# Computing two thirds of a mixer's gate projections inside another stage and passing them through DRAM

## The chip, the cores and the metric

The kernel runs on one core of a Trainium2 chip. The metric is the device time of one execution in microseconds (us): here the median of repeated runs.

## The reference

The reference is one inference step of a decoder trunk of two layers, for a prompt of 512 tokens and 8 single sample tokens, together 520 columns. A layer has a mixer with three parallel branches (retention, HGRN2, Mamba-2 SSD), merged by gates, and then a squared-ReLU MLP. What matters here:

```
proj = xn @ w_in                       # one big input projection, its last 3 x 1024 columns are the gates
...                                    # y_r, y_h, y_m: outputs of the three branches, 1024 wide each
ys     = stack([y_r, y_h, y_m])
branch = einsum('blnw,nwd->blnd', ys, w_branch)
gate   = sigmoid(gates.reshape(B, L, 3, 1024))
merged = sum(gate * branch, axis=2)
return merged @ w_out
```

A gate depends on the normalized input `xn` alone, and not on its branch, so that it can be computed at any time after `xn` and before its branch product.

## The kernel before

Activations are kept transposed: 128 features on the partitions, 520 tokens along the free axis, eight such blocks for 1024 features. Each float32 operand is held as two parts, high and low (`XN`, `YB`, and each weight); `mm3` (L209) makes a product from high x high, high x low and low x high, in two pieces of 256 and 264 columns. So one projection of 128 output features is 8 x 3 x 2 = 48 matmuls and needs one weight block of 512 KB. `wload` (L157) loads a block into one of four raw buffers and splits it in four pieces, each with one copy on ScalarE (L173) and one subtraction on VectorE (L174), into two ready pairs. The order of all weight uses is written down ahead in a list (L1190 and on), and `weights` (L182) starts loads up to four uses ahead.

`pj` (L233) gives a projection one of two accumulators in PSUM. The tile pool `up` has 18 buffers (tiles named `u`), shared by nearly all intermediate tiles of 128 x 520. The instructions of each engine are put in order before the run by a scheduler that goes by a model of time and by the order of the program; on the chip each engine, and SyncE's queue of transfers (SP), takes them in that fixed order.

One layer runs through these stages:

1. HGRN, eight heads. `hg_unit` (L487) is a generator of ten pieces. The first four start with a projection each: the forget gate (its exponentials follow), the query (ends at L561), the value (taken over at L580) and the output gate (L596). The other six (the products L630, the running state L632 and L634, the output L646, and so on) are issued as tails between the pieces of the next heads: `unit` (L270) runs one piece of the new head and then `step()` runs one piece of every tail.
2. SSD, four groups (`ssd_unit`, six pieces with a projection each, and six of tail).
3. `branch(l, 1, "first")` (L1080): for each of eight blocks, `gate` (L1072) projects the gate and takes it over with a tanh on ScalarE (L1074), then the branch product from `YB`, then gate times product on VectorE (L1090) into `T2`. Both halves end with a `step()`.
4. Retention, four heads (`ret_unit`, six pieces with a projection each, and four of tail), with the normalization of the SSD output as a tail.
5. `branch(l, 2, "mid")`: as 3, but the product is added to `T2` on GpSimd.
6. Eight gates of the first branch into `T1`, `branch(l, 0, "last")`, the output projection, the MLP.

Of the kernel before, what the change touches and what calls it, by code (L numbers as in the profile page):

```python
# [10 lines left out]
F32 = mybir.dt.float32  # L11
F32R = mybir.dt.float32r
U8 = mybir.dt.uint8
AF = mybir.ActivationFunctionType
ALU = mybir.AluOpType

P = 128
D = 1024
NB = 8
SEQ = 512  # L20
NS = 8
T = SEQ + NS
# [13 lines left out]
C_Z, C_XBC, C_DT, C_GATE = 7168, 8192, 10240, 10256  # L36
# [53 lines left out]
def hybrid_step(ctx: ExitStack, tc: tile.TileContext, x_prompt, x_sample, state_ret, state_hgrn, state_ssm,  # L90
# [5 lines left out]
    V, S, G, PE, SY = nc.vector, nc.scalar, nc.gpsimd, nc.tensor, nc.sync  # L96
# [7 lines left out]
    dp = ctx.enter_context(tc.tile_pool(name="dp", bufs=3, space=bass.MemoryType.DRAM))  # L104
# [5 lines left out]
    def nm(s):  # L110
        uid[0] += 1
        return f"{s}{uid[0]}"

    def ut(dt=F32):
        return up.tile([P, UW], dt, tag="u", name=nm("u"))[:, :T]
# [93 lines left out]
    def mm3(ps, w, ah, al, halves=(0, 1), m=P, ks=range(NB)):  # L209
        hi, lo = w  # L210
        for k in ks:
            for wt, act, st, sp_ in ((hi, ah, k == 0, False), (hi, al, False, False), (lo, ah, False, k == NB - 1)):
                for h in halves:
                    PE.matmul(ps[:m, CH[h]], lhsT=wt(k), rhs=act[:, k, CH[h]], start=st, stop=sp_)  # L214
# [18 lines left out]
    def pj():  # L233
        t = psj.tile([P, 1024], F32, tag="pj", name=nm("pj"))
        return t[:, 512 - CUTS[1]:512 - CUTS[1] + T]
# [6 lines left out]
    def w_cols(l, c0, n=128):  # L242
        return w_in[l, :, c0:c0 + n]

    def proj(l, c0, n=128):
        if (l, c0) in begun:
            ps = begun.pop((l, c0))
            mm3(ps, weights(w_cols(l, c0, n)), *XN, halves=(1,))
            return ps
        ps = pj()  # L250
        if (l, c0) in early:
            raw = early.pop((l, c0))
            mm3(ps, weights(w_cols(l, c0, n)), *YB, halves=(1,))
            scaled(raw, ps, 1)
            return raw
        mm3(ps, weights(w_cols(l, c0, n)), *XN, m=n)
        return ps
# [3 lines left out]
    def step():  # L261
        for g in list(tails):
            if next(g, "end") == "end":
                tails.remove(g)
# [2 lines left out]
        while tails:  # L267
            step()

    def unit(g, n):  # L270
        for _ in range(n):
            next(g)
            step()
        tails.append(g)

    def split(dst, val, scale=None, eng=None):
# [795 lines left out]
    def gate(l, b, d, dst):  # L1072
        ps = proj(l, C_GATE + 1024 * b + 128 * d)
        S.activation(out=dst, in_=ps, func=AF.Tanh, scale=0.5)  # L1074
        step()

    def w_br(l, b, d):
        return w_branch[l, b, :, 128 * d:128 * d + 128]

    def branch(l, b, mode):  # L1080
        for d in range(NB):
            if mode == "last":
                t = T1[:, d, :]
            else:
                t = ut()
                gate(l, b, d, t)
            ps = pj()
            mm3(ps, weights(w_br(l, b, d)), *YB)
            dst = T2[:, d, :] if mode == "first" else ut()
            V.scalar_tensor_tensor(out=dst, in0=t, scalar=1.0, in1=ps, op0=ALU.add, op1=ALU.mult)  # L1090
            if mode == "mid":
                G.tensor_tensor(out=T2[:, d, :], in0=T2[:, d, :], in1=dst, op=ALU.add)  # L1092
            elif mode == "last":
                V.tensor_tensor(out=dst, in0=T2[:, d, :], in1=dst, op=ALU.add)
                split((XN[0][:, d, :], XN[1][:, d, :]), dst, 0.5)
            step()
# [43 lines left out]
    def w_o(l, d):  # L1140
        return w_out[l, :, 128 * d:128 * d + 128]
# [7 lines left out]
    def hg_cols(h):  # L1149
        return [c + 128 * h for c in (C_HF, C_HQ, C_HI, C_HG)]  # L1150
# [18 lines left out]
    def add(src, n=128, store="w", start=None):  # L1169
        key = (str(src), len(key_info))  # L1170
        key_info[key] = (src, n, store if n == 128 else f"w{n}")
        fence[key] = len(uses) if start is None else start
        order.append(key)
        use(key)
        return key

    def use(key):
        first.setdefault(key, len(uses))
        last[key] = len(uses)
        uses.append(key)  # L1180
# [8 lines left out]
    for l in range(depth):  # L1189
        held = {}  # L1190
        for i, c in enumerate(early_cols if l else early_cols[:2]):
            held[c] = add(w_cols(l, c), store="wu"[i % 2] if l else "w")
        for h in range(HH):
            if h == HH - 1:
                add(w_cols(l, C_DT, 16), 16)
            for c in hg_cols(h):
                use(held[c]) if c in held else add(w_cols(l, c))
        for g in range(SG):
            for c in (C_XBC + 1024 + 128 * g, C_XBC + 1536 + 128 * g, C_XBC + 256 * g, C_XBC + 256 * g + 128,
                      C_Z + 256 * g, C_Z + 256 * g + 128):  # L1200
                add(w_cols(l, c))
        for d in range(NB):
            add(w_cols(l, C_GATE + 1024 + 128 * d))
            add(w_br(l, 1, d))
        for h in range(RH):
            for c in (C_RK + 128 * h, C_RQ + 128 * h, C_RV + 256 * h, C_RV + 256 * h + 128, C_RG + 256 * h,
                      C_RG + 256 * h + 128):
                add(w_cols(l, c))
        for d in range(NB):
            add(w_cols(l, C_GATE + 2048 + 128 * d))  # L1210
            add(w_br(l, 2, d))
        for d in range(NB):
            add(w_cols(l, C_GATE + 128 * d))
        for d in range(NB):
            add(w_br(l, 0, d))
        halves_order([w_o(l, d) for d in range(NB)], "y")
        for gi in range(4):
            held = {}
            for blocks, halves in up_order(gi):
                for i, d in enumerate(blocks):  # L1220
                    if halves == (1,) and d >= NUP - 4:
                        use(held[d])
                    else:
                        held[d] = add(w_u(l, gi, d), store="wu"[i % 2] if len(halves) == 1 else "w")
            if gi == 3:
                halves_order([w_d(l, gi, d) for d in range(NB)], "x")
            else:
                for d in range(NB):
                    add(w_d(l, gi, d))
# [18 lines left out]
    for c, (xt, (_, n)) in enumerate(zip(xts, rows)):  # L1248
# [9 lines left out]
        for i in range(2):  # L1258
# [3 lines left out]
            ps = pm()  # L1262
# [41 lines left out]
    for l in range(depth):  # L1304
        p = prms[l]
# [4 lines left out]
        else:  # L1310
            spare = [T2[:, i, :] for i in (0, 2, 7, 1)]
            for i, c in enumerate(early_cols):
                raw = spare[i]
                ps = pj()
# [8 lines left out]
        for h in range(HH):  # L1323
            if h == HH - 1:
                unit(ssd_dt(l, p, dtp), 1)
            unit(hg_unit(l, h, p), 4)
            if h == 1:
                G.memset(RR, 0.0)
        for g in range(SG):
# [22 lines left out]
        for gi in range(4):  # L1352
            for blocks, halves in up_order(gi):
                if gi == 0 and halves == (1,):
                    drain()
                for d in blocks:
                    ps = pj()
                    mm3(ps, weights(w_u(l, gi, d)), *XN, halves=halves)
                    c = slice(0, T) if len(halves) == 2 else CH[halves[0]]
                    n = c.stop - c.start  # L1360
                    a, t = ut()[:, :n], ut()[:, :n]
# [4 lines left out]
            for halves in ((0,), (1,)) if gi == 3 else ((0, 1),):  # L1366
                if gi == 3:
                    h = halves[0]
# [58 lines left out]
```

## Time and profile before

| | us |
|---|---|
| median of 3 runs | 2853.94 |
| lowest, highest | 2852.61, 2860.72 |
| profiled execution, its own time | 2847.65 |
| span of the profile | 2845.9 |

The span runs from the first to the last instruction in the trace; the profiled execution's own time is 1.75 us longer. In the stages named below, layer 0 has HGRN at 60 to 345 us, SSD at 345 to 538, the branch products of the second branch up to about 637; layer 1 has HGRN from about 1440 to 1740. PE is TensorE's matmul, PEld its weight load, DVE VectorE, ACT ScalarE, POOL GpSimd, SP the queue of SyncE.

### The profile page before, as it was taken

What the parts mean: (1) busy time and instruction counts of PE and PEld (TensorE: products, weight loads), DVE (VectorE), ACT (ScalarE), POOL (GpSimd) and SP (SyncE); (2) the same over time, 40 slices, a digit from 0 to 9 for tenths busy, and PEclk for the clock granted to TensorE, in tenths of its full rate; (3) what the DMA queues carried; (4) which work ended last, traced back from release to release, by engine and by line L of the source; (5) the groups of instructions that cost most, each with busy time, mean ns of one, the idle gap of its engine ahead of it and who ended that gap; (6) DMA issues with size and microseconds to landing.
All of it is one profiled execution on the core that took longest, in us unless ns stands there. A gap on an engine that the chain in (4) does not pass through costs nothing. (4 is left out here: it accounts for less than half of the span.)

```text
span 2845.9 us, 56632 instructions
## 1 busy us (share of the span) xinstructions
PE 2742.3 (96%) x22489; PEld 2652.0 (93%) x22489; DVE 1700.2 (60%) x3714; ACT 1168.6 (41%) x2858; POOL 738.1 (26%) x939
## 2 busy tenths in 40 slices
PE   5999899999999999999989999999999999999999
PEld 5888899999999999999978888999999999899998
DVE  4666799837654453443576668997476435534444
ACT  3444455424323353332444445553343234433333
POOL 2555443302211031000145554352022100300004
PEclk8999999999999999999999999999999999999999
DMA  5433355734543432333323333565354435133331
GB/s 145 118 102 103 88 143 149 179 90 122 162 126 96 123 87 80 96 90 90 109 70 106 106 107 93 140 171 147 90 156 133 123 95 149 45 97 90 95 97 63
DMA packets 597594, 317.99 MB, mean 112 GB/s; under 512 B 94385, under 2 KB 580273, under 8 KB 597201
## 3 DMA queue, kind: packets, MB, share of 16 engines
q1 hardware_dynamic: 596688, 314.21, 39.6%
q8 instruction: 178, 2.92, 0.4%
q14 instruction: 88, 0.71, 0.1%
q0 software_dynamic: 640, 0.15, 0.0%
HBM read 278.89 MB, written 35.41 MB: 110 GB/s over the span
## 5 line engine op out<-in xcount | busy, mean ns | idle before, releaser
L214 PE MATMUL pj<-XH,w 128*128 128x256 f32 (+1 forms) x8896 | 1529.7, 288 | 18.8 <-ACT T L580 6.0
L214 PEld LDWEIGHTS pj<-XH,w 128*128 128x128 f32 x8896 | 1268.7, 190 | 43.6 <-issue 10.9
L173 ACT ACTIVATE w<-wr 128x256 fp32r<-128x256 f32 (+1 forms) x1552 | 517.0, 404 | 1085.2 <-PE pj L214 1010.9
L214 PE MATMUL pj<-XL,w 128*128 128x256 f32 (+1 forms) x4448 | 947.2, 288 | 5.4 <-DVE XL L357 3.3
L174 DVE TENSOR_TENSOR w<-wr,w 128x256 fp32r<-128x256 f32 (+1 forms) x1552 | 630.7, 461 | 376.4 <-ACT w L173 375.8
L214 PEld LDWEIGHTS pj<-XL,w 128*128 128x128 f32 x4448 | 709.3, 190 | 19.4 <-issue 10.7
L214 PE MATMUL pj<-YH,w 128*128 128x256 f32 (+1 forms) x3456 | 575.4, 284 | 3.0 <-ACT YH L356 1.3
L214 PEld LDWEIGHTS pj<-YH,w 128*128 128x128 f32 x3456 | 487.6, 189 | 8.9 <-ACT w L173 3.4
L214 PE MATMUL pj<-YL,w 128*128 128x256 f32 (+1 forms) x1728 | 365.0, 284 | 2.5 <-DVE YL L357 2.4
L214 PEld LDWEIGHTS pj<-YL,w 128*128 128x128 f32 x1728 | 275.0, 189 | 5.0 <-DVE YL L357 4.0
L317 POOL TENSOR_TENSOR u<-u,u 128x256 f32<-128x256 f32 (+1 forms) x56 | 47.0, 840 | 567.7 <-ACT u L316 567.6
L1362 DVE SCALAR_TENSOR_TENSOR u<-pj,RR 128x520 f32<-128x520 f32 (+2 forms) x74 | 46.1, 625 | 171.8 <-PE pj L214 169.8
L933 POOL TENSOR_TENSOR u<-u,cst 128x520 f32<-128x520 f32 x16 | 22.0, 1376 | 292.8 <-ACT u L932 282.8
L1379 POOL TENSOR_SCALAR T<-T,gn 128x256 f32<-128x256 f32 (+1 forms) x16 | 16.0, 1003 | 298.9 <-ACT u L313 298.9
L1374 DVE TENSOR_TENSOR T<-T,pj 128x520 f32<-128x520 f32 x32 | 22.3, 696 | 115.3 <-PE pj L214 115.3
L287 PE MATMUL pm<-ident,u 128*128 128x128 f32 (+3 forms) x320 | 49.7, 276 | 20.5 <-DVE u L1260 20.4
L1092 POOL TENSOR_TENSOR T<-T,u 128x520 f32<-128x520 f32 x16 | 27.2, 1700 | 132.8 <-DVE u L1090 132.8
L287 PEld LDWEIGHTS pm<-ident,u 128*128 128x128 f32 (+3 forms) x320 | 37.3, 145 | 22.5 <-DVE u L1260 10.9
L287 PE MATMUL pm<-ident,T 128*128 128x128 f32 (+1 forms) x368 | 56.5, 281 | 1.3 <-DVE u L1134 1.0
L625 POOL TENSOR_TENSOR u<-u,s 128x512 f32<-128x512 f32 x32 | 37.5, 1188 | 66.5 <-DMA u<-in_state_hgrn_dram 52.8
L738 POOL TENSOR_TENSOR u<-u,u 128x544 f32<-128x544 f32 x32 | 45.7, 1428 | 34.5 <-DVE u L737 29.8
L648 ACT ACTIVATE u<-pm 128x512 f32<-128x512 f32 x16 | 9.5, 596 | 108.7 <-PE pm L646 108.7
(320 smaller groups left out, 3394.3 us busy)
## 6 DMA issues: line engine op xcount, KB each, us to landing
wr<-in_w_in_dram SPq DMA_DIRECT2D x208, 512.0 KB
wr<-in_w_up_dram SPq DMA_DIRECT2D x66, 512.0 KB
wr<-in_w_down_dram SPq DMA_DIRECT2D x64, 512.0 KB
u<-rbd SPq DMA_DIRECT2D x96, 256.0 KB
wr<-in_w_branch_dram SPq DMA_DIRECT2D x48, 512.0 KB
out_dram<-u SPq DMA_DIRECT2D x72, 256.0 KB
out_dram<-u SPq DMA_DIRECT2D x72, 128.0 KB
u<-in_state_hgrn_dram SPq DMA_DIRECT2D x32, 256.0 KB
```

What stands on the lines that cost most here:

```text
L173: a = S.activation(out=hi, in_=rq, func=AF.Copy)
L174: b = V.tensor_tensor(out=lo, in0=rq, in1=hi.bitcast(F32), op=ALU.subtract)
L214: PE.matmul(ps[:m, CH[h]], lhsT=wt(k), rhs=act[:, k, CH[h]], start=st, stop=sp_)
L287: PE.transpose(out, in_, ident[:k, :k])
L317: (eng or V).tensor_tensor(out=acc, in0=acc, in1=sq, op=ALU.add)
L625: G.tensor_tensor(out=c3(sts[i]), in0=c3(sts[i]), in1=bc(fs[:, s0, None], shc), op=ALU.mult)
L738: G.tensor_tensor(out=c, in0=c, in1=e, op=ALU.add)
L933: G.tensor_tensor(out=b, in0=b, in1=cst[:, K_SIN:K_SIN + T], op=ALU.mult)
L1092: G.tensor_tensor(out=T2[:, d, :], in0=T2[:, d, :], in1=dst, op=ALU.add)
L1362: V.scalar_tensor_tensor(out=a, in0=ps[:, c], scalar=0.0, in1=RR[:, c], op0=ALU.max, op1=ALU.mult)
L1374: V.tensor_tensor(out=T2[:, d, :], in0=T2[:, d, :], in1=ps, op=ALU.add)
L1379: G.tensor_scalar(out=T2[:, d, CH[h]], in0=T2[:, d, CH[h]], scalar1=p["fpost"][:, d:d + 1], scalar2=None, op0=ALU.mult)
```

## The change

The gates of the second and third branch (16 projections in each layer) are no longer computed in `branch`. They are computed in the HGRN stage: after the second and after the fourth piece of each head (with a few moved by one head in layer 1, where the first head uses another source for its projections). Each goes from PSUM through the tanh into a `u` tile and from there by a transfer of SP into a tile in DRAM. `branch` reads it back by a transfer of SP into a `u` tile in the place where it computed it. The list of weight uses follows. `branch` has one `step()` for each block in these two calls, where it had two.

```diff
-    def unit(g, n):
-        for _ in range(n):
+    def unit(g, n, after=None):
+        for i in range(n):
             next(g)
             step()
+            if after:
+                after(i)
         tails.append(g)
...
+    gates = {}
+
+    def gates_at(l, h, i):
+        at = {0: (3,), 1: (0, 1, 3)}.get(h, (1, 3)) if l else (1, 3)
+        n = 2 * h - (l > 0 and h == 1)
+        return [(1 + g // NB, g % NB) for g in (n + k for k, x in enumerate(at) if x == i)]
+
+    def gate_ahead(l, b, d):
+        ps = proj(l, C_GATE + 1024 * b + 128 * d)
+        t = ut()
+        S.activation(out=t, in_=ps, func=AF.Tanh, scale=0.5)
+        gates[l, b, d] = kept = dp.tile([P, T], F32, tag="gate", name=nm("gate"), bufs=2 * NB)
+        SY.dma_start(out=kept, in_=t)
+
...
             else:
                 t = ut()
-                gate(l, b, d, t)
+                SY.dma_start(out=t, in_=gates[l, b, d])
             ps = pj()
...
-            for c in hg_cols(h):
+            for i, c in enumerate(hg_cols(h)):
                 use(held[c]) if c in held else add(w_cols(l, c))
+                for b, d in gates_at(l, h, i):
+                    add(w_cols(l, C_GATE + 1024 * b + 128 * d))
...
         for d in range(NB):
-            add(w_cols(l, C_GATE + 1024 + 128 * d))
             add(w_br(l, 1, d))
...
         for d in range(NB):
-            add(w_cols(l, C_GATE + 2048 + 128 * d))
             add(w_br(l, 2, d))
...
-            unit(hg_unit(l, h, p), 4)
+            unit(hg_unit(l, h, p), 4, lambda i: [gate_ahead(l, *g) for g in gates_at(l, h, i)])
```

## Rows read from the trace of the kernel before

**Rows 1.** The page: busy time of all engines over the span.
```profile
PE 2742.3 (96%) x22489; PEld 2652.0 (93%) x22489; DVE 1700.2 (60%) x3714; ACT 1168.6 (41%) x2858; POOL 738.1 (26%) x939
```

**Rows 2.** Busy time in stretches: HGRN, SSD, second branch; then HGRN of layer 1.
```profile
core 0: us, PE busy (x) PEld busy (x) DVE busy (x) ACT busy (x) POOL busy (x), PEclk, DMA share, GB/s
60.00:345.00 285.00, 264.56 (x2186) 249.91 (x2185) 199.85 (x398) 131.00 (x283) 152.13 (x202) 0.96 0.38 106
345.00:538.00 193.00, 192.74 (x1587) 179.54 (x1586) 176.67 (x377) 102.55 (x234) 77.60 (x127) 1.00 0.58 148
580.00:630.00 50.00, 50.00 (x419) 50.00 (x418) 15.00 (x40) 13.77 (x39) 0.00 (x0) 1.00 0.34 94
840.00:900.00 60.00, 60.00 (x502) 60.00 (x501) 24.74 (x49) 18.19 (x51) 7.11 (x5) 1.00 0.33 90
...
1510.00:1740.00 230.00, 212.38 (x1791) 200.38 (x1790) 159.74 (x317) 105.46 (x224) 124.05 (x160) 0.98 0.36 102
```

**Rows 3.** TensorE's waits, HGRN of layer 0, 60 to 350 us: total, times, longest.
```profile
PE pm L646 <- DVE u L634: 10.5, 7, 1.8
PE pj L214 <- ACT T L580: 4.1, 1, 4.1
PE pj L214 <- DVE T L561: 3.1, 6, 0.6
PE pm L646 <- DVE u L632: 1.5, 1, 1.5
```

**Rows 4.** TensorE's waits, HGRN of layer 1, 1440 to 1780 us.
```profile
PE pm L646 <- DVE u L634: 9.1, 5, 1.8
PE pm L630 <- ACT u L621: 5.0, 4, 4.5
PE pm L646 <- DVE u L632: 3.1, 1, 3.1
```

**Rows 5.** Stretches of 10 us in HGRN, columns as in rows 2.
```profile
210.00:220.00 10.00, 8.17 (x57) 7.96 (x56) 6.39 (x12) 1.64 (x4) 5.54 (x7) 0.83 0.57 164
...
1500.00:1510.00 10.00, 5.47 (x33) 5.27 (x32) 9.47 (x14) 6.43 (x13) 9.54 (x15) 0.77 0.45 139
```

**Rows 6.** Instructions in order of time in one HGRN head, layer 0.
```profile
204.82 1.16 PE L630 MATMUL pm<-u,u 128*128 128x128 f32 x8 [0.20 <-ACT u L621]
...
209.90 2.21 DVE L174 TENSOR_TENSOR w<-wr,w 128x256 fp32r<-128x256 f32 x3
...
213.91 0.33 DVE L634 SCALAR_TENSOR_TENSOR u<-u,u,pm 128x128 f32<-128x128 f32 x1
...
214.30 0.49 PE L646 MATMUL pm<-u,T 128*128 128x128 f32 x2 [1.83 <-DVE u L634]
```

**Rows 7.** The same view at the last head of layer 0.
```profile
327.25 0.47 ACT L554 ACTIVATE u<-u 128x324 f32<-128x324 f32 x1 [2.93 <-POOL u L548]
...
330.01 0.80 PE L214 MATMUL pj<-XH,w 128*128 128x256 f32 x2 [4.13 <-ACT T L580]
```

**Rows 8.** VectorE in order of time in the second branch's products.
```profile
585.33 0.70 DVE L1090 SCALAR_TENSOR_TENSOR T<-u,pj 128x520 f32<-128x520 f32 x1 [4.20 <-PE pj L214]
...
596.86 0.70 DVE L1090 SCALAR_TENSOR_TENSOR T<-u,pj 128x520 f32<-128x520 f32 x1 [4.20 <-PE pj L214]
```

**Rows 9.** Groups by line over the span: the split of weights.
```profile
L174 DVE TENSOR_TENSOR w<-wr,w 128x256 fp32r<-128x256 f32 (+1 forms) x1552 | 630.7, 461 | 376.4 <-ACT w L173 375.8
...
L173 ACT ACTIVATE w<-wr 128x256 fp32r<-128x256 f32 (+1 forms) x1552 | 517.0, 404 | 1085.2 <-PE pj L214 1010.9
```

**Rows 10.** One line's instructions: the gates' tanh (ns, shortest, median, longest).
```profile
L1074 ACT ACTIVATE u<-pj x32: 579/584/589, 538.6 to 2301.6; 128x520 f32<-128x520 f32 x32
```

**Rows 11.** Where the SSD tails overlap the second branch, columns as in rows 2.
```profile
540.00:550.00 10.00, 10.00 (x92) 9.33 (x87) 9.01 (x17) 2.73 (x7) 7.81 (x7) 1.00 0.77 194
550.00:560.00 10.00, 10.00 (x94) 9.36 (x94) 7.88 (x19) 3.65 (x10) 3.93 (x3) 1.00 0.97 248
```

## Prediction

> **What bounds the kernel now.** I read the busy totals first, then busy time by stage, then TensorE's waits in each stage, and last the order of time around the longest repeated wait. The totals say that TensorE's matmuls cover 96% of the span and no other engine more than 60% [rows 1]. So the time is TensorE's work plus what it idles, and an edit that takes no matmul away can only gain from idle time and from a slow clock. The stages say where these are. In the second branch's products TensorE is busy for 50.00 of 50 us and in the third's for 60.00 of 60, at a granted clock of 1.00, and in SSD for 192.74 of 193 [rows 2]. In HGRN it is busy for 264.56 of 285 us at a mean clock of 0.96 (layer 0), and for 212.38 of 230 at 0.98 (layer 1) [rows 2]. That is 20.4 + 17.6 = 38.0 us of idle time. A mean clock of 0.96 over 285 us is worth 11.4 us of work at full clock, 0.98 over 230 us another 4.6: together 16.0. All the rest of the two layers' mixers has nothing to give.
>
> What TensorE waits for in HGRN is mostly one thing: the output product (L646), which needs the running state, a chain of short VectorE operations (L632, L634). It costs 10.5 + 1.5 us in layer 0 and 9.1 + 3.1 in layer 1, up to 1.8 us each in the steady heads [rows 3, 4]. The order of time shows why: the products into the state (L630) are issued at 204.82, but VectorE is at other work, a weight split of 2.21 us among it, and L634 runs at 213.91, and TensorE, which has taken what was ordered before the output, stands for 1.83 us [rows 6]. In such a stretch the mean clock is 0.83 [rows 5]. A second kind is an accumulator that is late to come free: 4.1 us once, where ScalarE stood behind an exponential that waited for GpSimd [rows 3, 7], and 3.1 us over six waits for the query [rows 3]. The first heads of layer 1 have one longer wait of 4.5 us, for L630 [rows 4], in a stretch where the clock is 0.77 [rows 5].
>
> **The change, part by part.**
>
> *Moved matmuls.* In the second branch two blocks follow each other by 11.53 us (585.33 to 596.86), with one gate and one product between [rows 8], so one projection is 5.77 us. 32 of them move: 184.6 us leave stages where TensorE is full, and each leaves with its whole length as long as nothing else there becomes the bound. 184.6 us enter HGRN. Net 0 before idle time is counted.
>
> *What the branch stages need without them.* A block then has 5.77 us of TensorE, and beside it one weight split (four pieces of 461 ns on VectorE, 1.84 us, and four of 404 ns on ScalarE, 1.62 us) [rows 9] and the product with the gate (0.70 us on VectorE) [rows 8]. That is 2.5 of 5.77 us: hidden. Weights come at the rate of before, one for each 5.77 us. A gate is 128 x 520 x 4 bytes, 266 KB, so a block moves 524 + 266 KB in 5.77 us, 137 GB/s, where the stage now moves 94 [rows 2] and 248 are seen elsewhere [rows 11]. The read is issued as each block comes and is needed 5.77 us later, so it is hidden; without that cover it would add its transfer, 1.1 us at 248 GB/s. The exception is the start of the second branch, where the last SSD tail loads and stores states: the transfer engines are busy for 0.77 and 0.97 of two stretches of 10 us [rows 11]. 20 us of further 46 GB/s are 0.92 MB, 3.7 us late at 248 GB/s; weights that are loaded ahead cover it, and without them it costs 3.7 us in each layer. `branch` now has 8 steps in a call where it had 16, but the tails in front need 6 (SSD) and 4 (retention), so no tail is left for the drain. The `T2` blocks that the last SSD group uses are overwritten from block 4 on; its last read comes in the sixth step, a block before block 6 writes there. If it is late, at most a block's time is lost, 5.8 us in each layer. Bounds for the branch stages: 0 to 2 x (3.7 + 5.8) = 19 us lost; I take 3, near the covered end, as TensorE has no gap there now.
>
> *What HGRN gets beside matmuls.* 16 splits more in each layer: 16 x 1.84 = 29 us of VectorE and 16 x (1.62 + 0.58) = 35 us of ScalarE (the tanh is 584 ns [rows 10]), while the stage grows by 92 us. VectorE goes from 199.85 of 285 to 229 of some 365, from 70% to 63%; ScalarE from 46 to 45%. Neither becomes the bound. The writes add 266 KB twice in a head to a stage at 106 GB/s, hidden. A `u` tile is held for the tanh and the write. SP's queue has the weight loads behind each write, and the write waits for the tanh; the raw weight buffers hold loads that are three blocks ahead, so a wait there is hidden while it is shorter than two or three blocks of 5.77 us.
>
> *The waits that are filled.* A gate after the second piece stands between the state products (L630, issued with that piece's tail) and the output (L646, with the next piece's tail). It gives VectorE 5.77 us more, where it was 1.83 us late. So the 24.2 us of L646's waits [rows 3, 4] should go; bounds 0 (the fixed order puts the output earlier as well) and 24.2. I take 20. The slow clock behind these waits in layer 0 goes with them: 0 to 11.4 us, I take 5, since some of it stands at the stage's last head, behind the 4.1 us wait, which I leave: there are still two projections between the forget gate and the query's release. In layer 1 the first head's wait gets one gate in front: 4.5 us and 0.23 of 10 us for the clock [rows 4, 5], 0 to 6.8; I take 4.
>
> *New waits.* The gate's accumulator is freed by a tanh in ScalarE's fixed order, which stands behind exponentials that wait for GpSimd. No such row exists; the nearest are the waits for the query's accumulator, 0.6 us at most and 3.1 us over six in layer 0, and the one of 4.1 us [rows 3]. 32 gates: 0 to 32 x 0.6 = 19 us (the 4.1 us case is a rival below). I take 5: most gates have 5.77 us of other matmuls before their accumulator is wanted.
>
> *Sum.* 20 + 5 + 4 - 5 - 3 = 21 us gained. The profiled execution, 2847.65 us, goes to 2826.7; the median of the runs is 6.3 us above it, and 2853.94 - 21 is 2833 us.
>
> **The rivals.**
>
> *All the room is filled.* Gates give TensorE other work at every wait. That is 38.0 us of idle time, 16.0 of clock and 6.8 at layer 1's first head: 60.8 us, 2793 us. For it: a gate can be taken up wherever two accumulators allow. Against it: with an order fixed beforehand a filler is only where the model of time put it, and the last head's wait is of another kind.
> The Trainium skill (Perfetto Trace Analysis, Identifying the Most-Contended Engine) says that matmul busy time misleads and that the room of TensorE is to be read from the busy share of weight loads. By the weight loads HGRN has 35.1 + 29.6 = 64.7 us open [rows 2], which would make 2789 us if all were filled. The trace speaks against it here: SSD has 13.5 us open in weight loads with matmuls busy to 0.26 us [rows 2].
>
> *The waits move.* The scheduler uses the added projections in its model's gaps and places the output product as tightly behind the state as before, or VectorE is later by the added split (1.84 us against a lateness of 1.83). Then L646 keeps its 24.2 us, the clock its 16, and only the first head's 4 us come, less the 3 of the branches: within 8 us of before, 2853 us. For it: all these waits are already the product of such a misjudged order [rows 6].
>
> *Slower: accumulators held.* Place: the two buffers of `pj` in HGRN. Tanh of a gate stands in ScalarE's order behind an exponential that waits 2.93 us for GpSimd, as at the last head, where TensorE lost 4.13 us [rows 7]. If each of 16 heads loses that once with its two gates, it is 66 us against the 29 gained: 37 us slower, 2891. It decides from 29 / 32 = 0.9 us for each gate; at 1.2 us the kernel is slower by over 0.3%. Against it: in the eight heads of layer 0 one such wait is seen [rows 3].
>
> **How the numbers follow.** About 0.3% (8.6 us) is what a measurement of this kernel can tell from no change. Forecast (9 to 45 us faster): 0.50. All the room: 0.14. The waits move: 0.20. Accumulators held: 0.16. So faster 0.64, same 0.20, slower 0.16. The likeliest case runs from 2809 to 2845. The range leaves out half of the full-room case and most of the slower one: 2800 to 2862.
>
> **What would show it.** Right: in HGRN TensorE's waits for L634 fall below 5 us over both layers and the mean clock of layer 0's stage is 0.98 or more; a block of the second branch takes 5.8 us from product to product with TensorE busy throughout; HGRN of layer 0 is some 75 us longer and not 92. Wrong: L634 stays at the head of TensorE's waits; a wait for the new tanh stands there with over 15 us; or TensorE has gaps in the second branch that end on a weight split, on a gate's read or on SSD's last operations.

## The result, and the profile after

The changed kernel takes 2809.6 us (median of 4 runs, 2808.62 to 2810.0); the kernel before, in the same comparison, 2853.28 us (4 runs, 2845.93 to 2860.72). The ratio is 0.9849, 95% interval 0.9832 to 0.9865: 43.7 us faster. Forecast were 21: the direction was right, the time lies inside the range, and the gain is just over twice the forecast. The profiled execution after took 2809.37 us, 38.3 less than the one before.

The page of the changed kernel, busy time over the span, beside [rows 1]:

```profile
PE 2727.6 (97%) x22489; PEld 2643.7 (94%) x22489; DVE 1713.1 (61%) x3714; ACT 1168.6 (42%) x2858; POOL 739.6 (26%) x939
```

The number of instructions of each engine is the same; only their places differ. Busy time in stretches of the changed kernel, columns as in [rows 2]; the first line is the stretch of HGRN that stands first there, the second one of layer 1 between first and last head, the third the last head of layer 0, the fourth the third branch:

```profile
60.00:345.00 285.00, 284.50 (x2450) 277.06 (x2448) 183.44 (x371) 133.18 (x302) 126.08 (x175) 1.00 0.46 128
1500.00:1750.00 250.00, 250.00 (x2169) 241.96 (x2168) 160.04 (x316) 114.82 (x260) 102.55 (x135) 1.00 0.42 118
380.00:400.00 20.00, 13.65 (x89) 12.78 (x90) 16.85 (x34) 8.26 (x18) 13.87 (x19) 0.74 0.24 68
855.00:880.00 25.00, 25.00 (x211) 25.00 (x210) 15.94 (x33) 7.72 (x21) 7.92 (x5) 1.00 0.44 128
```

Where TensorE was busy for 264.56 of 285 us at a mean clock of 0.96 it now is for 284.50 at 1.00. What is left of idle time in HGRN stands at the last heads, with the granted clock at 0.74 in layer 0's, and in layer 1 also at its start (3.8 and 2.1 us, 3.1 and 2.1 before). TensorE's waits of the changed kernel, layer 0's steady heads (60 to 360 us) first, then the lines on L648 of its whole span. The code has moved by two lines: L634, L636, L648 and L563 are what L632, L634, L646 and L561 were:

```profile
PE pj L214 <- DVE T L563: 0.3, 1, 0.3
PE pm L289 <- DVE u L1303: 0.2, 1, 0.2
...
PE pm L648 <- DVE u L634: 7.5, 2, 4.5
PE pm L648 <- DVE u L636: 6.6, 2, 3.6
```

The output product's waits are gone from the steady heads [rows 3, 4]; two are left in each layer, both in its last head. No wait for the new tanh (L1089) shows anywhere. TensorE in order of time in one steady head of layer 1 after (15 rows of the same projection are left out):

```profile
1625.45 1.05 PE L632 MATMUL pm<-u,u 128*128 128x128 f32 x8
1626.31 0.48 PE L214 MATMUL pj<-XH,w 128*128 128x256 f32 x2
...
1631.90 0.40 PE L214 MATMUL pj<-XH,w 128*128 128x256 f32 x2
1632.14 1.05 PE L505 MATMUL pm<-T 128*128 128x128 f32 x8
1633.03 1.06 PE L588 MATMUL pm<-T 128*128 128x128 f32 x8
1633.92 0.61 PE L646 MATMUL pm<-u,u 128*128 128x128 f32 x4
1634.37 0.39 PE L648 MATMUL pm<-u,T 128*128 128x128 f32 x2
```

Between the state products (L632) and the first output product (L648) now stand 48 matmuls, a whole projection, and L648 starts without a wait. Before, 14 matmuls of a projection stood in front of the first output product and 10 more in front of the second, which waited:

```profile
1649.51 1.16 PE L630 MATMUL pm<-u,u 128*128 128x128 f32 x8
1650.42 0.36 PE L214 MATMUL pj<-XH,w 128*128 128x264 f32 x1
1651.34 0.48 PE L214 MATMUL pj<-XH,w 128*128 128x256 f32 x2 [0.56 <-DVE T L561]
...
1656.89 0.28 PE L214 MATMUL pj<-XH,w 128*128 128x256 f32 x1
1659.00 0.49 PE L646 MATMUL pm<-u,T 128*128 128x128 f32 x2 [1.83 <-DVE u L634]
```

Where the 38.3 us between the two profiles are, in stretches from one fixed instruction to the next (the first forget gate's operation on VectorE, SSD's first and last convolution, the last branch product, and so on):

| stretch | layer 0, before to after | layer 1, before to after |
|---|---|---|
| HGRN | 298.8 to 368.4 | 293.2 to 364.1 |
| SSD | 166.8 to 167.9 | 167.1 to 168.1 |
| end of SSD to last product of the second branch | 110.9 to 66.0 | 110.8 to 66.0 |
| retention | 139.4 to 139.5 | 139.5 to 139.4 |
| third branch | 125.9 to 80.7 | 125.8 to 80.6 |
| first branch, output projection | 147.4 to 146.4 | 147.4 to 146.5 |
| MLP | 334.2 to 334.1 | 331.1 to 332.3 |

Sixteen projections of 5.77 us came into HGRN in each layer, 92.3 us; it grew by 69.6 and 70.9. So 22.7 + 21.4 = 44.1 us of the added work cost nothing. The rest of the kernel lost 5.8.

From head to head the growth is regular. The time between the same instruction of successive heads (VectorE's first operation on the forget gate, L517 before, L519 after) in layer 1, less 5.77 us for each gate between them: before 31.5, 34.7, 35.9, 35.9, 35.8, 35.8, 43.7; after 27.4, 32.5, 32.5, 32.5, 32.4, 32.5, 40.4. A steady head became 3.4 us shorter. In layer 0 three heads took 37.4 before, and they gained 4.9.

### The profile page after: what moved, and what is told of

Its sections match the earlier page's. It is cut to its first block, busy times and chain, and to the rows that moved or that the text cites. A ratio compares the mean times of both kernels' runs of the same rounds, so it can differ in the third digit from the quotient of the medians.

```text
span 2807.5 us, 56800 instructions
## 1 busy us (share of the span) xinstructions
PE 2727.6 (97%) x22489; PEld 2643.7 (94%) x22489; DVE 1713.1 (61%) x3714; ACT 1168.6 (42%) x2858; POOL 739.6 (26%) x939
## 3 DMA queue, kind: packets, MB, share of 16 engines
q1 hardware_dynamic: 605904, 331.25, 41.9%
## 4 chain that ended last, share of the span: by engine, by line
PE 87%; DVE 5%; DMA 3%; issue 2%; ACT 2%; POOL 1%; SPq 1%; POOLq 0%; DVEq 0%; ACTq 0%
PE pj L214 76%; PE pm L289 3%; PE pm L505 1%; DVE w L174 1%; PE pm L465 1%; PE pm L513 1%; ACT w L173 1%; DMA wr<-in_w_in_dram 1%; DMA u<-rbd 1%; DVE T L354 1%; PE pm L868 1%; PE pm L1035 0%; PE pm L1004 0%; PE pm L588 0%; PE pm L646 0%
## 5 line engine op out<-in xcount | busy, mean ns | idle before, releaser
L214 PE MATMUL pj<-XH,w 128*128 128x256 f32 (+2 forms) x8896 | 1509.1, 286 | 9.2 <-ACT XH L281 3.8
L214 PEld LDWEIGHTS pj<-XH,w 128*128 128x128 f32 (+1 forms) x8896 | 1259.0, 189 | 32.0 <-issue 12.2
L173 ACT ACTIVATE w<-wr 128x256 fp32r<-128x256 f32 x1552 | 517.1, 404 | 1106.8 <-PE pj L214 1006.4
L214 PE MATMUL pj<-XL,w 128*128 128x256 f32 (+2 forms) x4448 | 943.7, 287 | 5.3 <-DVE XL L359 3.2
L174 DVE TENSOR_TENSOR w<-wr,w 128x256 fp32r<-128x256 f32 x1552 | 657.6, 476 | 384.1 <-ACT w L173 383.7
L214 PEld LDWEIGHTS pj<-XL,w 128*128 128x128 f32 (+1 forms) x4448 | 705.9, 189 | 19.5 <-issue 10.7
L289 PE MATMUL pm<-ident,u 128*128 128x128 f32 (+3 forms) x320 | 49.9, 276 | 21.4 <-DVE u L1276 20.2
L627 POOL TENSOR_TENSOR u<-u,s 128x512 f32<-128x512 f32 x32 | 35.8, 1136 | 83.6 <-DMA u<-in_state_hgrn_dram 76.2
```

The lines of the kernel that those rows point to most:

```text
L173: a = S.activation(out=hi, in_=rq, func=AF.Copy)
L174: b = V.tensor_tensor(out=lo, in0=rq, in1=hi.bitcast(F32), op=ALU.subtract)
L289: PE.transpose(out, in_, ident[:k, :k])
L627: G.tensor_tensor(out=c3(sts[i]), in0=c3(sts[i]), in1=bc(fs[:, s0, None], shc), op=ALU.mult)
```

## Experiments

All the kernels of this section compute the whole reference. A "place" is the piece of a head behind which a gate stands, counted 0 to 3 (forget gate, query, value, output gate): the change has its two gates of a steady head at 1 and 3. The kernels that move gates differ from the change in `gates_at` alone, by a table of places for each head (its lists are written shorter here). That of the pair at 1 and 1:

```diff
-        at = {0: (3,), 1: (0, 1, 3)}.get(h, (1, 3)) if l else (1, 3)
-        n = 2 * h - (l > 0 and h == 1)
+        table = ([(1, 1)] * 8, [(3,), (1, 1, 1)] + [(1, 1)] * 6)[l]
+        at = table[h]
+        n = sum(len(t) for t in table[:h])
```

"Gap" is the time from head to head as above, with the gates in it (two in a steady head).

**The kernel before once more.** No edit.

> The kernel before once more, unchanged. Theory of the clock: its runs spread over 2846 to 2861 us because in some runs more HGRN heads fall to a slow TensorE clock behind the wait for the state (37.4 us from head to head instead of 35.9; three such gaps in the first profile, which took 2847.65 us). Then this profile shows about one more gap of 37.4 us for each 1.5 us that its time lies above 2847.65, and all of the difference lies in HGRN. Rival: the spread comes from elsewhere (transfers, start); then the gaps from head to head are as in the first profile whatever the time is.

It took 2854.15 us, 6.5 more than the profiled execution of before. The same stretch of layer 1's HGRN in the first profile of the kernel before, then in this one:

```profile
1580.00:1600.00 20.00, 18.19 (x161) 16.97 (x161) 13.41 (x28) 4.86 (x12) 11.72 (x12) 1.00 0.39 110
```

```profile
1580.00:1600.00 20.00, 18.17 (x148) 16.94 (x148) 13.94 (x28) 4.60 (x12) 11.05 (x11) 0.91 0.39 110
```

Busy and idle time agree, but the clock granted is 1.00 in one (2.4 GHz throughout) and 0.91 in the other (a part of it at 1.2 GHz), and 148 matmuls get done instead of 161. The gaps of layer 1 are 35.9 and then 37.4, 37.4, 37.4, 45.2 here, and were 35.9, 35.8, 35.8, 43.7: four heads of 1.5 us, 6.0 of the 6.5. With idle time of 1.8 us in each head, TensorE's clock dips in some heads of some executions and not in others. The first profile showed three such heads, this one seven; its time is the median of the kernel's runs beside it (2854.08).

**Both gates behind the query** (1 and 1, the diff above), **both behind the output gate** (3 and 3), **behind the forget gate and the value** (0 and 2):

> The changed kernel with both gates of a head after its second piece (layer 1: first head after its fourth, second head three after its second). Theory of the place (a gate helps where it stands between the state products and the output product): time as the changed kernel, 2805 to 2815 us, TensorE's waits for the state (the VectorE lines of the running state) gone in the steady heads. Theory of the filler (any added projection fills any wait): the same, 2805 to 2815. Together with the next two it tells them apart.

> The changed kernel with both gates of a head after its fourth piece, which is behind the output product in the order of the program. Theory of the place: the waits of the output product for the state come back, 15 to 24 us over both layers, with the slow clock behind some of them: 2826 to 2845 us. Theory of the filler: 2805 to 2815 us, and no such wait in the steady heads.

> The changed kernel with the gates of a head after its first and third piece, so that none is issued between the state products and the output product by the order of the program (layer 1: first head after its fourth piece, second head after its first, third and fourth). Theory of the place: most of the waits of the output product stay, 2822 to 2840 us. Theory of the filler: 2805 to 2815 us.

| places | us, median (range) | ratio to before, 95% | steady gap | less two gates |
|---|---|---|---|---|
| 1 and 1 | 2815.7 (2812.48 to 2817.24) | 0.9867 (0.985 to 0.9883) | 45.1 | 33.6 |
| 3 and 3 | 2843.18 (2842.43 to 2845.36) | 0.9965 (0.9952 to 0.9978) | 47.1 | 35.6 |
| 0 and 2 | 2806.94 (2806.27 to 2807.66) | 0.9834 (0.982 to 0.9849) | 44.8 | 33.3 |
| 1 and 3 (the change) | 2809.6 (2808.62 to 2810.0) | 0.9849 (0.9832 to 0.9865) | 44.0 | 32.4 |

The pair at 3 and 3 brings the same matmuls, splits and transfers into HGRN, and nearly nothing is gained: a steady head less its gates is 35.6 us, as before. TensorE's waits over its span, and its order in one head:

```profile
PE pm L648 <- DVE u L634: 22.3, 13, 4.2
...
PE pm L648 <- DVE u L636: 15.6, 13, 1.3
```

```profile
1607.43 1.05 PE L632 MATMUL pm<-u,u 128*128 128x128 f32 x8
...
1612.17 0.48 PE L214 MATMUL pj<-XL,w 128*128 128x256 f32 x2
1614.02 0.46 PE L648 MATMUL pm<-u,T 128*128 128x128 f32 x2 [1.37 <-DVE u L634]
...
1616.96 0.49 PE L648 MATMUL pm<-u,T 128*128 128x128 f32 x2 [1.30 <-DVE u L636]
```

Few matmuls stand between L632 and L648, as before the change, and the waits are as large. So it is not more work in the stage that fills the waits, but where in the head it stands. I had thought the pair at 0 and 2 too early and too late for that, and expected 2822 us at least; it came out at 2806.94, with 51 matmuls between L632 and L648 and no wait there in the steady heads. With 1 and 1 there are 97, and that pair's 2815.7 lies just above the 2805 to 2815 that were expected. Common to these three is one gate at least in front of the value's end, and in all three the value's projection stands behind L632 and covers VectorE's running state: ScalarE takes it over (L582) behind the matmuls that are counted here. That the gate in front gives the chain of exponentials the time to end in L632's operands is argued. The pair at 0 and 2 is the fastest of the table although its steady heads are longer than the change's: its last heads take 50.7 and 49.9 us, where the change has 54.3 and 53.4.

The second difference is the gate at 3. ScalarE in order of time in one head with the gates at 1 and 1, then in the change:

```profile
1616.30 0.60 ACT L518 ACTIVATE T<-pj 128x520 f32<-128x520 f32 x1
1617.78 0.38 ACT L515 ACTIVATE u<-pm 64x256 f32<-64x256 f32 x1 [0.87 <-PE pm L513]
1618.95 1.28 ACT L524 ACT_TABLE_LOAD   x1
...
1627.44 0.48 ACT L556 ACTIVATE u<-u 128x324 f32<-128x324 f32 x1 [1.55 <-POOL u L550]
```

```profile
1613.43 0.58 ACT L518 ACTIVATE T<-pj 128x520 f32<-128x520 f32 x1
1613.91 0.36 ACT L515 ACTIVATE u<-pm 64x256 f32<-64x256 f32 x1
1614.91 1.28 ACT L524 ACT_TABLE_LOAD   x1
...
1623.46 0.48 ACT L556 ACTIVATE u<-u 128x324 f32<-128x324 f32 x1 [1.38 <-POOL u L550]
```

From the forget gate's tanh (L518) to the exponential of L556 it takes 11.1 us at 1 and 1, and 10.0 in the change: without a gate behind the fourth piece, an older head's operation (L515) makes ScalarE wait 0.87 us for TensorE in the middle of the new head's chain. At 0 and 2 the same wait is 0.82 us and the chain 11.15; at 3 and 3 it is 10.0 again. The steady gaps of the two kernels without a gate at 3 are 0.8 and 1.1 us longer than the change's. The kernel before has no gate there either, and the same wait and chain (its L516, L513 and L554 are these lines):

```profile
1637.38 0.60 ACT L516 ACTIVATE T<-pj 128x520 f32<-128x520 f32 x1
1638.85 0.38 ACT L513 ACTIVATE u<-pm 64x256 f32<-64x256 f32 x1 [0.87 <-PE pm L511]
...
1648.49 0.47 ACT L554 ACTIVATE u<-u 128x324 f32<-128x324 f32 x1 [1.55 <-POOL u L548]
```

So a steady head has two gains, and each is a wait of TensorE that ends. A gate ahead of the value's end takes away the wait for the state, 1.83 us. The gate at 3, by ScalarE's shorter chain, takes away the wait for the query, 0.56 us, and a short one at the state products. With the gates at 1 and 1 these two still stand; with 3 and 3, which has the short chain, they are gone from the steady heads and the waits for the state stay. TensorE's waits in four steady heads of layer 1, for the query before, and all of them at 1 and 1 (in the change there are none):

```profile
PE pj L214 <- DVE T L561: 2.2, 4, 0.6
```

```profile
PE pj L214 <- DVE T L563: 2.2, 4, 0.6
PE pm L632 <- ACT u L623: 0.6, 4, 0.2
```

A wait costs more than the idle time that the profile records. A projection's matmuls start every 0.12 us, but each is recorded as lasting 0.27 to 0.39 us, and the idle time counts from that end. In the rows of the kernel before above, the starts on the two sides of the waits of 0.56 and 1.83 us lie 0.92 us (1650.42 to 1651.34) and 2.11 us (1656.89 to 1659.00) apart. Taken from start to start, less 0.12 us, the waits of a steady head of layer 1 cost 3.1 us before, 1.1 at 1 and 1, and nothing in the change. The 1.1 is nearly all by which a head at 1 and 1 is longer than the change's; at 0 and 2 it is 0.6 of 0.9, for waits of up to 0.2 us at L505. Of the 3.4 us of a steady head the waits are thus 3.1, and the rest are matmuls that start closer to each other without a wait.

**Half of the change:** only the second branch's gates ahead, at place 1; the third branch's stay where they were.

```diff
+        table = ([(1,)] * 8, [(), (1, 1)] + [(1,)] * 6)[l]
...
         for d in range(NB):
+            add(w_cols(l, C_GATE + 2048 + 128 * d))
             add(w_br(l, 2, d))
...
-                SY.dma_start(out=t, in_=gates[l, b, d])
+                if b == 1:
+                    SY.dma_start(out=t, in_=gates[l, b, d])
+                else:
+                    gate(l, b, d, t)
```

> Only the second branch's eight gates are computed ahead, one in each HGRN head after its second piece (layer 1: two in the second head, none in the first); the third branch computes its gates as before. What is taken to matter is that one projection more stands in front of the state products, so that the value's projection falls behind them and covers the state. Then one gate is as good as two: 2806 to 2820 us, no wait of 1.8 us for the state in the steady heads. Theory that the gain follows the amount of moved work: half of it, 2825 to 2836 us.

2824.35 us (2821.63 to 2826.04), ratio 0.9907 (0.9892 to 0.9922), between what was expected on either side. The steady gap is 39.4, 33.6 without its gate: what a head gains with both gates at 1 it gains with one of them there, and the waits for the query stand as they do there (2.2 us in four heads). In layer 1 the rest of the change's gain in HGRN is 11.9 us: 5.1 in the first head, which has no gate here and one at 3 in the change, and about 1.1 in each of the others but the last.

The half and the three kernels below were measured beside the kernel before, not beside the change; in ratio to the kernel before, the change stands at 0.9849.

**The transfers doubled:** every gate is written to a second tile and read from it too, in front of the true read.

```diff
+        again = dp.tile([P, T], F32, tag="again", name=nm("again"), bufs=2 * NB)
+        SY.dma_start(out=again, in_=t)
...
+                SY.dma_start(out=t, in_=gates[l, b, d, 1])
                 SY.dma_start(out=t, in_=gates[l, b, d])
```

> The changed kernel with every gate written to DRAM twice, into two tiles, and read back twice, one after the other. If the transfers are hidden: 2807 to 2816 us. Rival: the transfers cost what the branch stages lost against the moved matmuls (about 5 us), above all at the start of the second branch beside the states of the last SSD group; then it costs as much again or more, 2816 to 2830 us, with TensorE waits in that stretch.

2819.91 us (2817.68 to 2822.27), ratio 0.9894 (0.9877 to 0.991): some 10 more than the change. The steady heads of HGRN stay at 44.0, so 32 more writes there are hidden. The second branch's stretch takes 69.9 and 67.5 us (66.0 in the change) and the third's 85.7 and 85.2 (80.7), of which the stretch behind gives back 3.0 and 2.1. Doubled reads in the short blocks are not hidden. The second read goes into the same tile, and SP's queue waits until the first has landed (4.2 us in two waits around the second branch of layer 0), so how much of the 10 us is the transfer and how much this wait is not shown. For the single reads the loss of the branches in the change, below, is the bound.

**Two steps in a block:** the tails advance twice in each short block, as they did in the long ones.

```diff
                 SY.dma_start(out=t, in_=gates[l, b, d])
+                step()
             ps = pj()
```

> The changed kernel with a second step of the tails in each block of the second and third branch, as before the change, behind the read of the gate. If the halved pace of the tails is what costs the branch stages some us: 2803 to 2808 us. Rival: the pace is hidden, or the quicker tail crowds the start of the branch: 2808 to 2815 us.

2825.16 us (2821.77 to 2826.99), ratio 0.9909 (0.9895 to 0.9924): some 15 more than the change, which neither side expected. The branch stretches take 70.2, 70.5, 85.6 and 84.7 us, 17.7 more in all. TensorE waits for VectorE there (for L860, 1.3 and 0.6 us), and its weight loads are busy for 67.04 of the 75 us from 590 on, where the change has 69.48. Over these branches and the retention between them TensorE's recorded waits rise by only 3.1 us, and what makes up the rest of the 17.7 is not shown. The one `step()` for each block is a part of the change that earns its place.

**A third gate for the last head:** one from the first head of each layer goes to place 0 of the last.

```diff
+        table = ([(1,)] + [(1, 3)] * 6 + [(0, 1, 3)], [(), (0, 1, 3)] + [(1, 3)] * 5 + [(0, 1, 3)])[l]
```

> The changed kernel with one gate of each layer moved from the first head to the last, which gets three, after its first, second and fourth piece. In the changed kernel TensorE's longest waits of the HGRN stage are in the last head (4.5 and 3.0 us for the state in layer 0, 3.6 and 3.0 in layer 1, with a slow clock behind them). If a projection more before the state products covers these as it does in the steady heads: 2793 to 2804 us. Rival: these waits come from GpSimd and VectorE being late with the step size's chain, and remain, or the first head loses what the last gains: 2807 to 2816 us.

2810.94 us (2807.52 to 2813.09), ratio 0.986 (0.9845 to 0.9875): no difference from the change that can be told. TensorE's waits:

```profile
PE pj L214 <- ACT u L1090: 12.3, 2, 6.3
...
PE pm L632 <- ACT u L623: 4.5, 1, 4.5
```

The last head's waits for the running state are gone, and a wait for the gate's tanh (L1090 here) of up to 6.3 us has come in their place: that is the slower rival's mechanism, in the last heads alone. The second line is layer 1's first head, which lost its only gate: 4.5 us, as in [rows 4].

**The changed kernel once more**, on one chip with the three below:

> The changed kernel once more, on the chip of the three below, as their base. The clock theory (the kernel before has 1.8 us waits in each of its steady heads, and in some executions the clock dips in them and 1.5 us a head is added; the changed kernel has none of these waits) expects 2808 to 2811 us with a spread under 3 us, while the kernel before on this chip spreads over 5 to 15 us. If the spread of the kernel before has another cause, the changed kernel should spread as much.

2809.25 us (2809.12 to 2809.65), ratio 0.9856 (0.9842 to 0.9871). Its spread is 0.5 us, as expected; that of the kernel before on this chip is 3.7, under what was expected. The next kernel has no wait in its steady heads either and spreads over 4.3, so that the spread follows these waits is not shown.

**Gates behind the forget gate and the output gate** (0 and 3):

> The two gates of a head stand behind the first and the fourth piece instead of the third and the fourth. Theory of two places (a gate in any of the first three slots puts the value's projection behind the state products; a gate behind the fourth piece keeps the heads' ends apart from the next head's chain): both are met, so the steady gaps from head to head are 43.9 to 44.1 us as in the change, and the time is 2803 to 2812 us. Rival (only the place of the value's projection counts, and the pair behind the third and the fourth piece is better by something of its own): gaps of 44.8 us as with the pair behind the first and third piece, some 6 us more in each direction of that in the steady heads, 2808 to 2818 us.

2802.74 us (2800.51 to 2804.78), ratio 0.9836 (0.9819 to 0.9852), just under the 2803 to 2812 of the theory of two places. The steady gaps are 43.9 to 44.0, as the theory of two places has it, and L518 to L556 takes 10.0 us. The whole is 6.5 us under the change on the same chip, with ranges that don't meet. That gain is not in the steady heads: layer 0's last head takes 50.0 us where it took 54.2, its first gap is 41.4 and was 42.0, and layer 1's last head 52.3 and was 53.6. Its waits and clock in that head:

```profile
PE pj L214 <- ACT u L1090: 6.3, 1, 6.3
```

```profile
380.00:400.00 20.00, 15.88 (x123) 15.35 (x124) 16.50 (x35) 7.52 (x17) 12.09 (x19) 0.83 0.30 85
```

One wait of 6.3 us stands there where the change has two, of 4.5 and 3.0, and the mean clock is 0.83 instead of 0.74.

**The step-size unit in a middle head.** The last head of each layer has SSD's step sizes prepared in it, a unit with long VectorE operations on 16 partitions (L692 to L707). It is moved to stand in front of head 4:

```diff
-            if h == HH - 1:
+            if h == 4:
                 unit(ssd_dt(l, p, dtp), 1)
```

> The change with the unit that prepares SSD's step sizes moved from the last head of each layer to the one in front of head 4. Theory: the waits of 7.5 and 6.6 us of the last heads, and the clock of 0.74 in them, come from that unit's long operations on 16 partitions, which stand in VectorE's and GpSimd's queues in front of the head's own chain; in a middle head the added matmuls cover some of it. Then the last heads' gaps fall from 52 to 44 to 47 us and head 4's rises by less, and the time is 2790 to 2803 us. Rival (the unit delays whichever head it stands in by as much): head 4's gap rises to 50 to 52 us, the waits stand there, and the time is 2805 to 2815 us.

> Both of the two edits: gates behind the first and the fourth piece, and the step-size unit in front of head 4. If both theories hold, 2788 to 2803 us, and the lower of the three; if the places count for nothing beyond the value's projection, the same as the step-size edit alone plus some 6 us; if the unit's delay only moves, 2803 to 2815 us.

2807.89 us (2805.05 to 2810.75), ratio 0.9852 (0.9837 to 0.9866); with the gates at 0 and 3 besides, 2801.63 (2799.85 to 2804.07), 0.983 (0.9815 to 0.9845). The rival is right: the delay only moves. In layer 0 the gaps are 42.3, 44.0, 44.0, 51.9, 54.1, 44.0, 44.0 and the last head 44.0, where the change has 52.0 and 54.3 at the end. Busy time and clock around head 4, with the unit there:

```profile
250.00:270.00 20.00, 15.47 (x108) 14.60 (x109) 17.32 (x35) 8.35 (x19) 13.14 (x18) 0.74 0.24 61
```

```profile
PE pm L648 <- DVE u L634: 4.4, 1, 4.4
PE pm L648 <- DVE u L636: 3.0, 1, 3.0
```

These are the last head's waits and clock, in the middle of the stage. That the unit brings them is shown, and that a head there covers them no better than the last one. With the gates at 0 and 3 the head behind the unit takes 50.1 and 50.6 us in the two layers, where it takes 54.1 and 53.4 with the change's places: what that pair gains over the change, it gains in the head that the unit delays. The fastest two, 2802.74 and 2801.63, have ranges that overlap: either is some 7 us under the change.

## Why the forecast was right in direction and short by half

The forecast was a sum of 21 us. What the runs put in its place:

| term | forecast | measured |
|---|---|---|
| waits that are filled, L646's and the first head's (with its clock), less the new waits; measured as recorded idle time | 20 + 4 - 5 = 19 | 25.9 |
| what waits cost beyond the recorded idle time | not in the sum | 5.8 |
| slow clock, forecast for layer 0, measured in both layers | 5 | 8.4 |
| matmuls that start closer to each other without a wait | not in the sum | 4.0 |
| branches and the rest | -3 | -5.8 |
| median runs against the two profiled executions | not in the sum | 5.4 |
| sum | 21 | 43.7 |

The measured terms come from the whole HGRN stretch, before and after, layer 0 and layer 1:

```profile
55.50:353.70 298.20, 277.76 (x2305) 262.59 (x2303) 208.06 (x416) 139.22 (x301) 155.56 (x206) 0.97 0.38 105
1464.80:1757.40 292.60, 264.31 (x2199) 250.17 (x2198) 210.35 (x408) 140.12 (x297) 160.79 (x207) 0.96 0.34 95
```

```profile
55.50:423.30 367.80, 358.69 (x3064) 346.90 (x3063) 237.77 (x483) 169.61 (x385) 154.49 (x206) 0.99 0.43 120
1444.30:1807.80 363.50, 349.75 (x2965) 338.62 (x2964) 243.47 (x476) 170.31 (x381) 159.59 (x207) 0.97 0.39 112
```

TensorE idles for 20.4 + 28.3 us before and 9.1 + 13.8 after: 25.9 less. The next two terms are added up from the trace, matmul by matmul. Measured from start to start, less 0.12 us, the waits cost 56.7 us before and 25.0 after, 31.7 less, which is 5.8 beyond the idle time. The granted clock, as 1 minus its value times the time outside the waits, costs 17.9 us before and 9.5 after: 8.4 less. Of 44.1 that leaves 4.0. Matmuls that start more than 0.16 us after the one ahead of them, at full clock and without a wait, were 267 before and are 217 after, and cost 4.3 us less; what sets them is not shown.

*The step that failed* is the size of the room, in "What bounds the kernel" and "The waits that are filled". The room was read from recorded idle time, and of the waits in it only L646's and the first head's went into the sum. The waits for the query (L561), named there with 3.1 us in layer 0, were put at nothing without a reason. Over both layers they come to 5.8 us before, and after the change 0.3 is left of them outside the last heads. L630's short waits, 1.6 us, went with them. These two, 7.1 us, are about what lies between 19 and 25.9. Then each wait costs more than its recorded idle time (5.8 us), the clock was sized for layer 0 alone (8.4 against 5), and matmuls start closer together (4.0). That the room is in TensorE's waits and its clock was right; 40.1 of the 44.1 us are there.

I had set aside a rule for this. The Trainium skill (Perfetto Trace Analysis, Identifying the Most-Contended Engine) says to judge TensorE's room not by matmul busy time but by the weight loads' busy share, beside the share of peak FLOPs. By the weight loads HGRN had 35.6 + 42.4 us open, and 20.9 + 24.9 after: 32.2 less, near to the 31.7 us of the waits from start to start, where the matmuls' idle time fell by 25.9. The trace agrees with the rule in this stage. My argument against it came from SSD, which nothing had been moved into and so could not tell.

*New waits.* Five us were taken for accumulators that the tanh frees late. In the steady heads of layer 0 all of TensorE's waits come to 0.5 us. The loss stands at the last heads instead: less their gates, 42.8 and 41.9 us against 40.7 and 39.8 before, 2.1 in each layer; the recorded waits of the last heads rise from 11.6 to 16.5 us. It is not the tanh there but L648's wait for the running state, so that 5 us was near is luck. The rival that had TensorE wait for the tanh named a real mechanism, but it shows only in the last heads of other placements, at 6.3 us, and never in 16 heads.

*The clock.* The sum was made against an execution that had three dipped heads in layer 0 and none in layer 1. The median run of before lies 5.6 us higher, which a further four heads of 1.5 us explain in the one such execution that was profiled. The changed kernel has no wait in its steady heads, its two profiled executions show no such dips in them, and its first runs lie within 1.4 us of each other. I added the profile's gain to the median without asking what made the two differ.

*The waits that are filled* had the wait for the state right in place and size: the 19.6 us of it in the steady heads are gone. The reason was another. I wrote that a gate after the second piece gives VectorE 5.77 us more. What it does is to let the value's projection stand behind L632; a gate after the first piece does the same. *The waits move* is what the pair at 3 and 3 does: its 2843.18 us lies 10 below the 2853 of that rival.

*The branch stages* are as forecast but for the size. Where no tail's matmuls stand between, blocks follow each other by 5.77 us; the second branch shows one gap, of 1.24 us, behind SSD's last tail:

```profile
630.79 0.44 PE L871 MATMUL pm<-u,s 128*64 128x128 f32 x4
632.46 0.48 PE L214 MATMUL pj<-YH,w 128*128 128x256 f32 x2 [1.24 <-DVE T L1106]
```

By the table of stretches the branches lost 4.5 us in four passes (44.9 + 44.8 + 45.2 + 45.2 shorter, where four times 46.15 left), SSD 2.1, the MLP 1.1, and the first branch gave 1.9 back.

Of the signs to look for: the clock of layer 0 is 0.99, and HGRN of layer 0 is 69.6 us longer, near the 75 given. The waits for L634 (now L636) are 6.6 us and not under 5, all in last heads.

## What to carry to other kernels

Where instructions run in an order fixed beforehand, work moved into a stage fills its waits only if it pushes the right thing behind the wait's start: the same gates gave 44 us in one place and 11 in another, so look for what stands between the late producer's trigger and its consumer, and try two or three places. Recorded idle time was less here than what the waits cost, as a matmul is recorded past the moment at which the next can start; read the starts on both sides of a wait, the weight loads and the time from one repeat to the next as well, and give every wait on the list a line in the sum. Before a gain is subtracted from a median, find out how the profiled execution differs from the median run.

## What the runs showed of the hardware that was not expected

The same heads, with the same waits of 0.56 and 1.83 us, took 35.9 us in one execution and 37.4 in another, by the granted clock alone (1.00 and 0.91 in the same 20 us). So heads with waits this short took 1.5 us more in some executions, and the changed kernel's steady heads, without these waits, did not in either of its two profiles. A recorded wait of 1.83 us set the starts of two matmuls 2.11 us apart, where they follow each other by 0.12. Thirty-two more reads of 266 KB, each ahead of another into the same tile, cost some 10 us where a block takes 5.77 us; 32 more writes in heads of 44 us cost nothing that shows in their gaps.
